# Up projection's two activation parts in one 512-column product, with a third of its weight parts left on VectorE

## The chip, the cores and the metric

The kernel runs on one core of a Trainium2 chip. The metric is device time in microseconds (us) of one execution. Engines are named as in the profile: PE is TensorE's products, PEld its weight loads, DVE is VectorE, ACT is ScalarE, POOL is GpSimd, SP issues most of the DMAs.

## The reference

Two decoder layers on 256 tokens of width 1024, all in float32. Each layer has token mixers, a gated merge, a convolutional feed-forward block and a per-layer embedding. The change sits in the feed-forward block:

```python
def conv_ffn(u, w_up, conv_w, conv_b, w_down):
    up = u @ w_up
    pad = jnp.pad(up, ((0, 0), (CONV_W - 1, 0), (0, 0)))
    length = up.shape[1]
    conv = conv_b + sum(pad[:, j:j + length] * conv_w[j] for j in range(CONV_W))
    gate, val = jnp.split(conv, 2, axis=-1)
    return (jax.nn.gelu(gate, approximate=True) * val) @ w_down

# in each layer, D_MODEL = 1024, D_FF = 2816, CONV_W = 3
h = h + conv_ffn(rms_norm(h, g_ffn_norm[i]), w_up[i], conv_w[i], conv_b[i], w_down[i])
```

So `w_up` is 1024 x 5632, and each of its 5632 output columns is convolved over the tokens with three taps and a bias. The first half goes through a GELU and multiplies the second.

## The kernel before

Every large product is made of three products of the type float32r: an operand x is kept as hi + lo, where hi is x rounded to that type and lo the remainder, and x times w becomes hi(x) hi(w) + lo(x) hi(w) + hi(x) lo(w).

**Weights.** A layer's weights come as 128 chunks of 128 x 1024 numbers (`raw`, 512 KB). `split_hi` makes `wh` on ACT (L159), `split_lo` makes `wl = raw - wh` on DVE (L166), and then the next chunk's DMA is issued on SP. There are 5 `raw` buffers and 7 of each part. `prepare` keeps the parts up to 5 chunks ahead of use; it is called from `tick`, which is called after each group of products, so a chunk's parts stand in the instruction streams of ACT and DVE between the evictions of chunks that are used earlier. Every engine works through its stream in the order written.

**Activations.** A class `HL` holds hi and lo of a [128, 8, 256] operand (k of eight, 256 tokens) in separate tiles.

**Up projection.** It takes chunks 54 to 97 of a layer, 44 chunks: for each of 22 blocks `fb` of 128 columns, one chunk of the gate half (s = 0) and one of the value half (s = 1). A chunk's 8 k give 24 products of 256 columns (L827, L828, L829) into one of 4 PSUM tiles `tp`. Then ACT makes the last tap and the bias (L832), DVE adds the two shifted taps straight from PSUM (L834, twice), ACT applies the GELU to the gate half (L840), DVE multiplies the halves (L841), and ACT and DVE make hi and lo of the result (L846, L847), which the down projection uses as its stationary operand. A PSUM tile is free once the second L834 of its chunk is done, so PE can be at most four chunks ahead of DVE.

**Before it** come the output projection, whose second half ends with the norm of the feed-forward block (`ev_n`: sums of squares on ACT, three small instructions on POOL L265 to L267, two scalings `un` on DVE L783, for each of two token tiles), the transposes `ffn_T` on PE (L789) and the split of `u` (L791, L792). The small product with the embedding's projection runs between these steps. **After it** comes the down projection with 512-column products (L881 to L883).

Of the kernel before, what the change touches and what calls it, by code (L numbers as in the profile page):

```python
# [17 lines left out]
P = 128  # L18
# [90 lines left out]
def decoder_kernel(ctx: ExitStack, tc: tile.TileContext, x, pT, ws, fc, tb, gf, rope, out):  # L109
# [53 lines left out]
    def split_lo():  # L163
        raw = raws.pop(nx["lo"])
        wh, wl = parts[nx["lo"]]
        nc.vector.tensor_sub(wl, raw, wh.bitcast(F32))  # L166
        side.work(dve=1.12)
# [4 lines left out]
    def split_piece(a, n):  # L172
        """Columns a to a + n of the next chunk."""
# [12 lines left out]
    def prepare(n_lo, n_hi):  # L186
        """Have the parts of the chunks before n_lo and n_hi emitted."""
# [65 lines left out]
    def sq_half(ss, hf, tiles=(0, 1)):  # L253
        """ss[hf][:, i] = sum of h^2 / D over half of the columns."""
# [18 lines left out]
    class HL:  # L273
        """fp32r parts hi + lo of [128, 8, 256] operands, stored by halves of the k index."""

        def __init__(self, name, n=2):
            self.h = [b4(name + "h", F32R) for _ in range(n)]
            self.l = [b4(name + "l", F32R) for _ in range(n)]

        def hi(self, k):  # L280
            return self.h[k // 4][:, k % 4, :]

        def lo(self, k):
            return self.l[k // 4][:, k % 4, :]

    def split_T2(srcs, hf, k0, scale, x, between=None):
        """Parts (columns k0, k0 + 1 of half hf of x) of the transpose of two [128, 512] tiles; the scale is
        one for all k or a function of k."""
        hi, lo = x.h[hf][:, k0:k0 + 2, :], x.l[hf][:, k0:k0 + 2, :]
# [58 lines left out]
    def tables(l, t):  # L348
        """Tables of the layer: rope with gains, lambda, sub-norm gain."""
# [30 lines left out]
    def rope_rows(dst, src, n, tabs, i, dup=False):  # L380
        """dst, src [128, n, 64]"""
# [19 lines left out]
    def transposed(srcs, nb, dst):  # L401
        """dst [128, nb, 256] from two token-major [128, nb*128] tiles."""
# [9 lines left out]
    def stacked(q3):  # L412
        """fp32r [128 t, n, 2, 64] of [128 t, n, 64]: the two parts of each head side by side."""
# [6 lines left out]
    def transposed_parts(srcs, dsts):  # L420
        """[128, n, 256] (in tiles of 4) from two stacked [128 t, n, 128]."""
# [20 lines left out]
    for l in range(DEPTH):  # L442
# [120 lines left out]
        def heads_side(pr, nm, is_q):  # L563
            """Rope of eight heads, transposed; 1/rms beside the queries, in the keys."""
# [28 lines left out]
        def maps(qn, product, i, hq, mk):  # L593
            """Four masked score maps, exp'd, [128 t, 4, S]; head 4 hq + 2 m + r."""
# [21 lines left out]
        def ptrans(src, nh, i):  # L616
            """[128 s, nh * blocks, 128 t] of [128 t, nh, S]."""
# [69 lines left out]
        def mixer_a(hq, i):  # L687
# [20 lines left out]
            hi, lo = (t[0][:, 2 * hq:2 * hq + 2, i * P:(i + 1) * P] for t in (x.h, x.l))  # L708
# [61 lines left out]
        pxs = HL("px", 1)  # L770
# [5 lines left out]
        def ev_n(i, acc):  # L776
            """Second half of the columns of a token tile, then its norm for the ffn."""
# [8 lines left out]
        def ffn_T(i, hf):  # L786
# [3 lines left out]
            hi, lo = (t[hf][:, :, i * P:(i + 1) * P] for t in (u.h, u.l))  # L790
            nc.scalar.activation(hi, pt, AF.Copy)  # L791
            nc.vector.tensor_sub(lo, pt, hi.bitcast(F32))  # L792

        for hf in range(2):
# [227 lines left out]
```

## Time and profile before

| | |
|---|---|
| median of 3 timed executions | 800.34 us (798.68 to 802.0) |
| span of the profiled execution | 798.6 us |
| PE busy | 789.2 us, 99% of the span |
| DVE, ACT, POOL busy | 605.8 us (76%), 477.8 us (60%), 63.2 us (8%) |
| mean granted TensorE clock | 1.000 |

The profiled execution is known by its span, from its first to its last instruction; the timed executions lie 0.1 to 3.4 us above that. PE's busy time says that products stood in its pipeline nearly always. How fast they go through is read from the distance between the starts of two of them.

### The profile page before, as it was taken

What the parts mean: (1) busy time and instruction counts of PE and PEld (TensorE: products, weight loads), DVE (VectorE), ACT (ScalarE), POOL (GpSimd) and SP (SyncE); (2) the same over time, 40 slices, a digit from 0 to 9 for tenths busy, and PEclk for the clock granted to TensorE, in tenths of its full rate; (3) what the DMA queues carried; (4) which work ended last, traced back from release to release, by engine and by line L of the source; (5) the groups of instructions that cost most, each with busy time, mean ns of one, the idle gap of its engine ahead of it and who ended that gap; (6) DMA issues with size and microseconds to landing.
All of it is one profiled execution on the core that took longest, in us unless ns stands there. A gap on an engine that the chain in (4) does not pass through costs nothing.

```text
span 798.6 us, 12832 instructions
## 1 busy us (share of the span) xinstructions
PE 789.2 (99%) x4801; PEld 690.7 (86%) x4801; DVE 605.8 (76%) x1084; ACT 477.8 (60%) x843; POOL 63.2 (8%) x87
## 2 busy tenths in 40 slices
PE   8999999999999999999999999999999999999997
PEld 6877887788999999888888778878899999998887
DVE  6988986777888888754687889778688888884643
ACT  6767658366666666553566486575476666663541
POOL 0250300010000000000123212000100000000000
PEclk9999999999999999999999999999999999999999
DMA  8644463574555555656464335445555555567421
GB/s 324 205 158 134 132 211 106 172 235 135 185 185 185 184 185 180 228 172 225 133 201 162 125 121 188 154 132 191 190 160 184 185 185 186 184 190 259 162 102 53
DMA packets 40334, 139.58 MB, mean 175 GB/s; under 512 B 4560, under 2 KB 5968, under 8 KB 40272
## 3 DMA queue, kind: packets, MB, share of 16 engines
q1 hardware_dynamic: 39408, 136.91, 52.0%
q10 hardware_dynamic: 864, 1.84, 0.7%
q8 instruction: 38, 0.62, 0.3%
q14 instruction: 24, 0.20, 0.1%
HBM read 137.69 MB, written 1.05 MB: 174 GB/s over the span
## 4 chain that ended last, share of the span: by engine, by line
PE 93%; DVE 2%; POOL 1%; ACT 1%; DMA 1%; issue 1%; SPq 0%; DVEq 0%; ACTq 0%; POOLq 0%
PE acc L335 12%; PE acc L337 12%; PE acc L336 12%; PE tp L828 11%; PE tp L827 11%; PE tp L829 11%; PE acc L883 5%; PE acc L881 5%; PE acc L882 5%; PE tp L298 2%; PE tp L626 1%; PE tp L634 1%; POOL rq L251 1%; PE tp L705 1%; PE tp L639 1%; PE tp L605 1%
## 5 line engine op out<-in xcount | busy, mean ns | idle before, releaser
L166 DVE TENSOR_TENSOR wl<-raw,wh 128x1024 fp32r<-128x1024 f32 x254 | 306.2, 1219 | 25.9 <-ACT wh L159 25.4
L159 ACT ACTIVATE wh<-raw 128x1024 fp32r<-128x1024 f32 x254 | 264.7, 1057 | 38.8 <-PE acc L883 30.1
L828 PE MATMUL tp<-ul,wh 128*128 128x256 f32 x704 | 199.4, 283 | 0.0
L827 PE MATMUL tp<-uh,wh 128*128 128x256 f32 x704 | 199.4, 283 | 0.0
L829 PE MATMUL tp<-uh,wl 128*128 128x256 f32 x704 | 199.2, 283 | 0.0
L828 PEld LDWEIGHTS tp<-ul,wh 128*128 128x128 f32 x704 | 135.1, 192 | 0.1
L827 PEld LDWEIGHTS tp<-uh,wh 128*128 128x128 f32 x704 | 135.1, 192 | 0.0
L829 PEld LDWEIGHTS tp<-uh,wl 128*128 128x128 f32 x704 | 135.1, 192 | 0.0
L335 PE MATMUL acc<-wh,uh 128*128 128x512 f32 (+1 forms) x336 | 133.7, 398 | 0.0
L337 PE MATMUL acc<-wh,ul 128*128 128x512 f32 (+1 forms) x336 | 130.6, 389 | 0.0
L336 PE MATMUL acc<-wl,uh 128*128 128x512 f32 (+1 forms) x336 | 130.3, 388 | 0.0
L834 DVE SCALAR_TENSOR_TENSOR cv<-tp,fc,cv 128x255 f32<-128x255 f32 (+1 forms) x176 | 84.9, 483 | 40.2 <-ACT cv L832 37.0
L832 ACT ACTIVATE cv<-tp,fc 128x256 f32<-128x256 f32 x88 | 49.6, 564 | 90.0 <-PE tp L829 90.0
L337 PEld LDWEIGHTS acc<-wh,ul 128*128 128x128 f32 x336 | 63.1, 188 | 12.9
L335 PEld LDWEIGHTS acc<-wh,uh 128*128 128x128 f32 x336 | 63.2, 188 | 11.8 <-issue 0.3
L336 PEld LDWEIGHTS acc<-wl,uh 128*128 128x128 f32 x336 | 63.2, 188 | 11.6 <-DVE wl L166 0.2
L881 PE MATMUL acc<-wh,gh 128*128 128x512 f32 x176 | 68.9, 391 | 0.0
L883 PE MATMUL acc<-wh,gl 128*128 128x512 f32 x176 | 68.5, 389 | 0.0
L882 PE MATMUL acc<-wl,gh 128*128 128x512 f32 x176 | 68.5, 389 | 0.0
L265 POOL TENSOR_SCALAR sst<-ss 128x2 f32<-128x2 f32 (+1 forms) x8 | 5.6, 699 | 513.0 <-ACT junk L257 512.9
L611 ACT ACTIVATE pe<-tp,nb,rq 128x256 f32<-128x256 f32 (+1 forms) x64 | 31.8, 523 | 17.4 <-DVE nb L608 13.6
L883 PEld LDWEIGHTS acc<-wh,gl 128*128 128x128 f32 x176 | 33.0, 188 | 6.9
(185 smaller groups left out, 1018.9 us busy)
## 6 DMA issues: line engine op xcount, KB each, us to landing
raw<-ws SPq DMA_DIRECT2D x254, 512.0 KB, 3.4
raw<-ws SPq DMA_DIRECT2D x4, 256.0 KB, 5.0
gb<-gf ACTq DMA_DIRECT2D x2, 512.0 KB, 4.5
h<-x SPq DMA_DIRECT2D x2, 256.0 KB, 4.1
h<-x SPq DMA_DIRECT2D x1, 512.0 KB, 6.4
px<-pT ACTq DMA_DIRECT2D x2, 256.0 KB, 2.6
out<-h SPq DMA_DIRECT2D x2, 256.0 KB, 2.0
out<-h SPq DMA_DIRECT2D x4, 128.0 KB, 1.7
```

The source lines that it names most:

```text
L159: nc.scalar.activation(wh, raw, AF.Copy)
L166: nc.vector.tensor_sub(wl, raw, wh.bitcast(F32))
L335: nc.tensor.matmul(o, a, wh, start=q == 0, stop=False)
L336: nc.tensor.matmul(o, a, wl, start=False, stop=False)
L337: nc.tensor.matmul(o, b, wh, start=False, stop=q == nk - 1)
L827: nc.tensor.matmul(pu, wh[:, k, :], u.hi(k), start=k == 0, stop=False)
L828: nc.tensor.matmul(pu, wh[:, k, :], u.lo(k), start=False, stop=False)
L829: nc.tensor.matmul(pu, wl[:, k, :], u.hi(k), start=False, stop=k == KD - 1)
L834: nc.vector.scalar_tensor_tensor(c[:, sh:], pu[:, :L - sh], w[:, 2 - sh:3 - sh], c[:, sh:], op0=ALU.mult, op1=ALU.add)
L881: nc.tensor.matmul(acc[i], a, wh, start=k == 0, stop=False)
L882: nc.tensor.matmul(acc[i], a, wl, start=False, stop=False)
L883: nc.tensor.matmul(acc[i], b, wh, start=False, stop=k == NF - 1)
```

## The change

`HL` now keeps hi and lo of one k side by side, so that both are one operand of 512 columns (`pair`). In the up projection, the products of `wh` with hi and with lo become one product into a whole PSUM bank: its left half collects the terms of hi, its right half those of lo. The product of `wl` with hi goes on adding to the left half. Then the halves have to be added: ACT copies the right half to SBUF (`cl`), and DVE adds it to the left half, in place in PSUM. The last tap and the bias stay on ACT for the gate half and go to DVE for the value half. Of the 44 chunks of an up projection, the `wl` of 30 are made on POOL and those of 14 stay on DVE. In `ffn_T` each split becomes two, of two k each.

```diff
+    def on_pool(c):
+        return C_UP <= c < C_DN and (c - C_UP) % 3 != 2
...
     def split_lo():
         raw = raws.pop(nx["lo"])
         wh, wl = parts[nx["lo"]]
-        nc.vector.tensor_sub(wl, raw, wh.bitcast(F32))
-        side.work(dve=1.12)
+        if on_pool(nx["lo"] % NCHUNK):
+            nc.gpsimd.tensor_tensor(wl, raw, wh.bitcast(F32), op=ALU.subtract)
+        else:
+            nc.vector.tensor_sub(wl, raw, wh.bitcast(F32))
+            side.work(dve=1.12)
...
     class HL:
-        def __init__(self, name, n=2):
-            self.h = [b4(name + "h", F32R) for _ in range(n)]
-            self.l = [b4(name + "l", F32R) for _ in range(n)]
+        def __init__(self, name, n=KD):
+            self.t = [b4(name, F32R).rearrange("p (k a) t -> p k a t", a=2) for _ in range(n // 2)]
...
+        def pair(self, k):
+            return self.t[k // 2][:, k % 2, :, :]
...
         def ffn_T(i, hf):
...
-            nc.scalar.activation(hi, pt, AF.Copy)
-            nc.vector.tensor_sub(lo, pt, hi.bitcast(F32))
+            for k in (0, 2):
+                hi, lo = u.two(4 * hf + k, slice(i * P, (i + 1) * P))
+                nc.scalar.activation(hi, pt[:, k:k + 2, :], AF.Copy)
+                nc.vector.tensor_sub(lo, pt[:, k:k + 2, :], hi.bitcast(F32))
...
-                pu = ps_tp.tile([P, 512], F32, name="tp")[:, :L]
+                acc = ps_tp.tile([P, 2, L], F32, name="tp")
+                pu = acc[:, 0, :]
                 for k in range(KD):
-                    nc.tensor.matmul(pu, wh[:, k, :], u.hi(k), start=k == 0, stop=False)
-                    nc.tensor.matmul(pu, wh[:, k, :], u.lo(k), start=False, stop=False)
+                    nc.tensor.matmul(acc, wh[:, k, :], u.pair(k), start=k == 0, stop=False)
                     nc.tensor.matmul(pu, wl[:, k, :], u.hi(k), start=False, stop=k == KD - 1)
                 c = sm.tile([P, L], F32, name="cv", **T2)
+                cl = sm.tile([P, L], F32, name="cl", bufs=3)
                 w = cw[:, s * NF + fb, :]
-                nc.scalar.activation(c, pu, AF.Identity, bias=w[:, 3:4], scale=w[:, 2:3])
+                nc.scalar.activation(cl, acc[:, 1, :], AF.Copy)
+                nc.vector.tensor_add(pu, pu, cl)
+                if s:
+                    nc.vector.tensor_scalar(c, pu, w[:, 2:3], w[:, 3:4], op0=ALU.mult, op1=ALU.add)
+                else:
+                    nc.scalar.activation(c, pu, AF.Identity, bias=w[:, 3:4], scale=w[:, 2:3])
```

DVE's stream in the middle of an up projection, one block before: L834 are the taps of one chunk, L841 the product of the halves, L847 the lo part of the block ahead, L166 a weight part.

```order
L834 SCALAR_TENSOR_TENSOR cv<-tp,fc_76,cv 128x255
L834 SCALAR_TENSOR_TENSOR cv<-tp,fc_76,cv 128x254
L847 TENSOR_TENSOR gl<-cv,gh 128x256
L166 TENSOR_TENSOR wl<-raw,wh 128x1024
L834 SCALAR_TENSOR_TENSOR cv<-tp,fc_76,cv 128x255
L834 SCALAR_TENSOR_TENSOR cv<-tp,fc_76,cv 128x254
L166 TENSOR_TENSOR wl<-raw,wh 128x1024
L841 TENSOR_TENSOR cv<-cv 128x256
```

The same block now, one of those with a weight part left (L173): L849 adds the halves, L851 is the value half's last tap, L855 are the shifted taps, L868 the lo part, L862 the product of the halves.

```order
L849 TENSOR_TENSOR tp<-tp,cl 128x256
L855 SCALAR_TENSOR_TENSOR cv<-tp,fc_76,cv 128x255
L855 SCALAR_TENSOR_TENSOR cv<-tp,fc_76,cv 128x254
L868 TENSOR_TENSOR g<-cv,g 128x256
L173 TENSOR_TENSOR wl<-raw,wh 128x1024
L849 TENSOR_TENSOR tp<-tp,cl 128x256
L851 TENSOR_SCALAR cv<-tp,fc_76 128x256
L855 SCALAR_TENSOR_TENSOR cv<-tp,fc_76,cv 128x255
L855 SCALAR_TENSOR_TENSOR cv<-tp,fc_76,cv 128x254
L862 TENSOR_TENSOR cv<-cv 128x256
```

Of the two weight parts of a block 14/22 of one is left on average; two adds and one tap came in. In three blocks one has its part here, one in front of L862, one has none.

ACT's stream in one block now: L848 copies the right half, L853 is the gate half's last tap, L867 the hi part, L163 a weight part, L861 the GELU.

```order
L848 ACTIVATE cl<-tp 128x256
L853 ACTIVATE cv<-tp,fc_76 128x256
L867 ACTIVATE g<-cv 128x256
L163 ACTIVATE wh<-raw 128x1024
L848 ACTIVATE cl<-tp 128x256
L163 ACTIVATE wh<-raw 128x1024
L861 ACTIVATE cv<-cv 128x256
```

Before, each L848 here was an L832, and L853 did not exist. The value half's L848 stands behind a weight part of 1024 columns.

POOL's stream at the start of an up projection, now: L272 to L274 are the norm's three instructions for one token tile, L171 is a weight part.

```order
L272 TENSOR_SCALAR sst<-ss_1835 128x1
L273 TENSOR_TENSOR sst<-sst,ss_1836 128x1
L274 TENSOR_TENSOR rstd<-sst,mhalf 128x1
L171 TENSOR_TENSOR wl<-raw,wh 128x1024
L272 TENSOR_SCALAR sst<-ss_1835 128x1
L273 TENSOR_TENSOR sst<-sst,ss_1836 128x1
L274 TENSOR_TENSOR rstd<-sst,mhalf 128x1
L171 TENSOR_TENSOR wl<-raw,wh 128x1024 x29
```

Before, the six norm instructions (L265 to L267) stood there alone. The 30 weight parts are new: one between the two token tiles, 29 behind.

## Rows read from the trace of the kernel before

**Rows 1.** The page: busy us of each engine, share of the span, instructions.
```profile
PE 789.2 (99%) x4801; PEld 690.7 (86%) x4801; DVE 605.8 (76%) x1084; ACT 477.8 (60%) x843; POOL 63.2 (8%) x87
```
**Rows 2.** The chain that ended last, share of the span by line.
```profile
PE acc L335 12%; PE acc L337 12%; PE acc L336 12%; PE tp L828 11%; PE tp L827 11%; PE tp L829 11%; PE acc L883 5%; PE acc L881 5%; PE acc L882 5%; PE tp L298 2%; PE tp L626 1%; PE tp L634 1%; POOL rq L251 1%; PE tp L705 1%; PE tp L639 1%; PE tp L605 1%
```
**Rows 3.** Both up projections as stretches: busy us (instructions), PEclk, DMA share, GB/s.
```profile
190.00:317.00 127.00, 127.00 (x1058) 126.90 (x1058) 106.31 (x174) 81.78 (x134) 0.00 (x0) 1.00 0.57 186
583.00:710.00 127.00, 127.00 (x1060) 126.92 (x1059) 106.28 (x174) 81.76 (x133) 0.00 (x0) 1.00 0.57 185
```
**Rows 4.** Timeline of PE, up projection: start us, us, instruction.
```profile
230.02 0.28 PE L827 MATMUL tp<-uh,wh 128*128 128x256 f32 x1
...
230.38 0.28 PE L827 MATMUL tp<-uh,wh 128*128 128x256 f32 x1
```
**Rows 5.** Timeline of PE, down projection.
```profile
340.61 0.39 PE L881 MATMUL acc<-wh,gh 128*128 128x512 f32 x1
...
341.29 0.39 PE L881 MATMUL acc<-wh,gh 128*128 128x512 f32 x1
```
**Rows 6.** Groups of DVE by form: busy us, mean ns | idle before.
```profile
L166 DVE TENSOR_TENSOR wl<-raw,wh 128x1024 fp32r<-128x1024 f32 x254 | 306.2, 1219 | 25.9 <-ACT wh L159 25.4 <-issue 0.3
L834 DVE SCALAR_TENSOR_TENSOR cv<-tp,fc,cv 128x255 f32<-128x255 f32 x88 | 42.5, 483 | 37.0 <-ACT cv L832 37.0
L841 DVE TENSOR_TENSOR cv<-cv 128x256 f32<-128x256 f32 x44 | 18.4, 419 | 1.1 <-ACT cv L840 1.1
L847 DVE TENSOR_TENSOR gl<-cv,gh 128x256 fp32r<-128x256 f32 x44 | 18.3, 416 | 1.0 <-ACT gh L846 1.0
L710 DVE TENSOR_TENSOR ol<-tp,oh 128x256 fp32r<-128x256 f32 x8 | 3.4, 424 | 11.6 <-ACT oh L709 11.6
L695 DVE TENSOR_SCALAR pe<-pe,rcp 128x256 f32<-128x256 f32 x16 | 4.6, 349 | 0.1
```
**Rows 7.** Groups of ACT by form.
```profile
L159 ACT ACTIVATE wh<-raw 128x1024 fp32r<-128x1024 f32 x254 | 264.7, 1057 | 38.8 <-PE acc L883 30.1 <-DMA raw<-ws 8.6
L832 ACT ACTIVATE cv<-tp,fc 128x256 f32<-128x256 f32 x88 | 49.6, 564 | 90.0 <-PE tp L829 90.0
L840 ACT ACTIVATE cv<-cv 128x256 f32<-128x256 f32 x44 | 17.8, 405 | 0.0
L709 ACT ACTIVATE oh<-tp 128x256 fp32r<-128x256 f32 x8 | 3.1, 384 | 12.0 <-PE tp L705 12.0
```
**Rows 8.** Timeline of ACT and DVE, up projection, one chunk: [idle before <-releaser].
```profile
230.58 0.57 ACT L832 ACTIVATE cv<-tp,fc 128x256 f32<-128x256 f32 x1 [1.06 <-PE tp L829]
...
231.18 1.00 DVE L834 SCALAR_TENSOR_TENSOR cv<-tp,fc,cv 128x255 f32<-128x255 f32 x2 [0.41 <-ACT cv L832]
...
232.10 1.22 DVE L166 TENSOR_TENSOR wl<-raw,wh 128x1024 fp32r<-128x1024 f32 x1
...
233.23 0.42 DVE L841 TENSOR_TENSOR cv<-cv 128x256 f32<-128x256 f32 x1
```
**Rows 9.** Timeline of DVE and POOL at the end of the output projection.
```profile
172.02 1.22 DVE L166 TENSOR_TENSOR wl<-raw,wh 128x1024 fp32r<-128x1024 f32 x1
...
172.27 1.02 POOL L265 TENSOR_SCALAR sst<-ss 128x1 f32<-128x1 f32 x1 [74.84 <-ACT junk L257]
```
**Rows 10.** Timeline of POOL in the attention stage.
```profile
82.32 0.20 POOL L250 TENSOR_SCALAR pw<-hss 128x8 f32<-128x8 f32 x1 [26.94 <-DVE hss L398]
```
**Rows 11.** Groups of POOL by form.
```profile
L242 POOL CAST identr<-ident 128x128 fp32r<-128x128 f32 x1 | 0.3, 294 | 0.0
...
L250 POOL TENSOR_SCALAR pw<-oss 128x2 f32<-128x2 f32 x8 | 1.5, 192 | 8.1 <-DVE oss L670 6.5 <-ACT pt L627 1.2
```
**Rows 12.** Timeline of DVE and PE ahead of the first up projection.
```profile
185.40 1.42 DVE L783 SCALAR_TENSOR_TENSOR un<-h,rstd,gb 128x512 f32<-128x512 f32 x2 [1.77 <-POOL rstd L267]
...
189.51 0.60 PE L789 MATMUL tp<-ident,un 128*128 128x128 f32 x4
```
**Rows 13.** DMA issues: KB each, median us from issue to landing.
```profile
raw<-ws SPq DMA_DIRECT2D x254, 512.0 KB, 3.4
```

More of the change, by code (lines that the diff above doesn't have):

```diff
@@ L273, in decoder_kernel, with two @@
     class HL:
-        def __init__(self, name, n=2):
-            self.h = [b4(name + "h", F32R) for _ in range(n)]
-            self.l = [b4(name + "l", F32R) for _ in range(n)]
+        def __init__(self, name, n=KD):
+            self.t = [b4(name, F32R).rearrange("p (k a) t -> p k a t", a=2) for _ in range(n // 2)]
         def hi(self, k):
-            return self.h[k // 4][:, k % 4, :]
+            return self.t[k // 2][:, k % 2, 0, :]
         def lo(self, k):
-            return self.l[k // 4][:, k % 4, :]
+            return self.t[k // 2][:, k % 2, 1, :]
+        def pair(self, k):
+            return self.t[k // 2][:, k % 2, :, :]
+        def two(self, k, cols=slice(0, L)):
+            return (self.t[k // 2][:, :, a, cols] for a in range(2))
     def split_T2(srcs, hf, k0, scale, x, between=None):
-        hi, lo = x.h[hf][:, k0:k0 + 2, :], x.l[hf][:, k0:k0 + 2, :]
+        hi, lo = x.two(4 * hf + k0)
         n = 1 if callable(scale) else 2
@@ L707, in mixer_a @@
             x = o_parts()
-            hi, lo = (t[0][:, 2 * hq:2 * hq + 2, i * P:(i + 1) * P] for t in (x.h, x.l))
+            hi, lo = x.two(2 * hq, slice(i * P, (i + 1) * P))
             nc.scalar.activation(hi, po, AF.Copy)
@@ L769, in decoder_kernel @@
         ss = new_ss()
-        pxs = HL("px", 1)
+        pxs = HL("px", 2)
         u = HL("u")
@@ L789, in ffn_T @@
                 nc.tensor.transpose(pt[:, k, :], un[i][:, hf, k * P:(k + 1) * P], ident)
-            hi, lo = (t[hf][:, :, i * P:(i + 1) * P] for t in (u.h, u.l))
-            nc.scalar.activation(hi, pt, AF.Copy)
-            nc.vector.tensor_sub(lo, pt, hi.bitcast(F32))
+            for k in (0, 2):
+                hi, lo = u.two(4 * hf + k, slice(i * P, (i + 1) * P))
+                nc.scalar.activation(hi, pt[:, k:k + 2, :], AF.Copy)
+                nc.vector.tensor_sub(lo, pt[:, k:k + 2, :], hi.bitcast(F32))
         for hf in range(2):
@@ L800, in decoder_kernel @@
             if hf:
-                nc.scalar.activation(pxs.h[0][:, 0:2, :], px, AF.Copy)
-                nc.vector.tensor_sub(pxs.l[0][:, 0:2, :], px, pxs.h[0][:, 0:2, :].bitcast(F32))
+                pxh, pxl = pxs.two(0)
+                nc.scalar.activation(pxh, px, AF.Copy)
+                nc.vector.tensor_sub(pxl, px, pxh.bitcast(F32))
                 gemm_a(m, range(KD), stream(l, C_OUT + 4), 512, ev_n, {13: lambda: ffn_T(0, 0)}, outer=KD)
@@ L836, in decoder_kernel @@
                 cc.append(c)
-                side.work(pe=2.6)
-                side.work(dve=0.8, act=0.8)
+                side.work(pe=2.5)
+                side.work(dve=1.4 + 0.3 * s, act=1.1 - 0.5 * s)
                 tick()
@@ L841, in decoder_kernel, with parts_g @@
             nc.vector.tensor_mul(cc[1], cc[1], cc[0])
-            if fb % 4 == 0:
-                gx.append(HL("g", 1))
-            def parts_g(c=cc[1], ghi=gx[-1].hi(fb % 4), glo=gx[-1].lo(fb % 4)):
+            if fb % 2 == 0:
+                gx.append(HL("g", 2))
+            def parts_g(c=cc[1], ghi=gx[-1].hi(fb % 2), glo=gx[-1].lo(fb % 2)):
                 nc.scalar.activation(ghi, c, AF.Copy)
@@ L878, in decoder_kernel @@
                 for i in range(2):
-                    a = gx[k // 4].hi(k % 4)[:, i * P:(i + 1) * P]
-                    b = gx[k // 4].lo(k % 4)[:, i * P:(i + 1) * P]
+                    a = gx[k // 2].hi(k % 2)[:, i * P:(i + 1) * P]
+                    b = gx[k // 2].lo(k % 2)[:, i * P:(i + 1) * P]
                     nc.tensor.matmul(acc[i], a, wh, start=k == 0, stop=False)
```

## The prediction

> **What bounds the kernel now.** I read the page first: PE is busy 99% of the span [rows 1]. That says little of its pace, so I went to the chain that ended last: nearly all of it is products, and the three lines of the up projection have 11% each, a third of the time [rows 2]. The two stretches of it, 127 us each, show PE busy throughout at full clock, DVE at 106 us of 127, ACT at 82, POOL at nothing [rows 3]. So these stages go at PE's pace. It is read from starts: three 256-column products take 0.36 us, 120 ns each [rows 4]; three 512-column ones of the down projection take 0.68 us, 226.7 ns each [rows 5]. A chunk of 24 products takes 2.88 us, a block of two 5.76. In it, ACT idles 1.06 us until PE is done with the chunk, and DVE then 0.41 us until ACT is [rows 8]: both wait for PE, not PE for them. That is what the change may spend.
>
> **PE's part.** Doubling the columns adds 106.7 ns, which is 256 columns at 2.4 GHz; so each product carries 13.3 ns that do not depend on columns. Per k, two products of 120 become one of 226.7 and the third stays: 346.7 instead of 360. For 8 k and 88 chunks that is 704 x 13.3 = **9.4 us less**, and a chunk takes 2.77 us, a block 5.55, a layer's up projection 122. The operand's weights are loaded beside a longer product than before, so I add nothing for loads. The Trainium skill ("TensorE: Matmul & The Clock Gate", Back-to-back issue gap) gives columns over 2.4 GHz plus 2.5 ns as the gap between isolated warm products; by it 704 x 2.5 = 1.8 us would be saved. Rows 4 and 5 do not agree with that gap, and the sum goes by the rows.
>
> **DVE's block without POOL.** Lengths overlap a little from one instruction to the next, so I take distances between starts: the two taps 0.92, a weight part 1.13 [rows 8], and for 256-column ones without a wait the length less 0.08, so 0.34 [rows 6]. New in it are two adds from PSUM, nearest row L710, 424 ns, and one last tap: 349 ns is a scaling from SBUF, 483 one with two inputs [rows 6], I take 0.42. Neither row writes PSUM; I come back to that. Handing over between engines, or between an instruction and one of the same engine that needs it, costs 0.03 to 0.04: L832 ends at 231.15, the tap starts at 231.18 [rows 8].
> Gate half: add 0.42, then DVE stands while ACT makes the last tap, 0.56 [rows 7] and two handovers, 0.07; taps 0.91; lo part 0.34. That is 2.30.
> Value half: add 0.46, last tap 0.46, taps 0.91, multiply 0.34: 2.17.
> Weight parts: 14/22 x 1.13 = 0.72.
> Also, ACT reaches the value half's copy (0.384 by L709) only behind hi part and weight part [rows 7]: 0.45 + 0.47 + 0.30 + 0.95 + 0.38 = 2.55 us after the gate half's add began, while DVE is there after 2.30. So it waits 0.29 in the two of three blocks that have no weight part in front: 0.19. Sum: **5.38 of 5.55 us**. ACT's own work (two weight parts, two copies, last tap, GELU, hi part) is under 4.3 us. DVE fits, with 0.17 us per block, 3.7 us per layer; before, its waits for ACT alone were 0.8 per block [rows 8]. Besides, four PSUM tiles let DVE fall behind: three chunks of 2.77 are 8.3 us, less the 2.5 us that a chunk's chain takes anyway, 5.8 us per layer.
>
> **POOL's part.** 30 weight parts per layer. No row shows a long two-input instruction on POOL. A cast of 128 columns takes 294 ns, one of 2 columns 192 [rows 11]: 0.81 ns per column, 1.02 us for 1024 read once. Two operands read in turn: 0.19 + 2 x 0.83 = 1.85 us. I keep 1.02 and 1.85 as bounds and take 1.85, since there are two operands. (The Trainium skill, "GPSIMD Engine Reference", Elementwise side-by-side, measured 4497 ns for 2048 columns, an estimate of 2.25 us here; no run here shows it, and the sum below would come to about 840 us.) POOL then has 30 x 1.85 = 55 us of work in 122, 45%.
>
> **Where POOL and DVE meet.** A POOL instruction issued at 172.27, 0.25 us into a weight part of DVE that ran from 172.02 to 173.24, took 1.02 us and ended at 173.29, just behind it [rows 9]. One of the same kind on eight times the columns, right behind the reduction on DVE that it had waited for, took 0.20 [rows 10]. So while DVE streams two inputs from SBUF, POOL does not get through. Whether DVE stands likewise while POOL reads, no row shows: POOL's reads are too short. I forecast that it does. The Trainium skill ("SBUF — State Buffer", Who interferes with whom) says so: DVE with two SBUF inputs and a reading GpSimd exclude each other for whole instructions, whoever comes first. Rows 9 agree for the one order.
> DVE has 22 multiplies, 22 lo parts and 14 weight parts per layer with two SBUF inputs (the taps and adds have one in PSUM): 58. If each meets a busy POOL 45% of the time and then waits half of 1.85, that is 58 x 0.42 = 24.4 us per layer. Off it go 3.7 and 5.8 us from above, and 1.9 where the lo part's wait falls into the 0.29 that DVE waits for the copy anyway (22 x 2/3 x 0.29 x 0.45). **13.0 us per layer remain, 26 in all**: multiply and taps behind the caught instruction come late, PSUM tiles come free late, and PE stands. Both bounds: at 1.02 us the waits are 58 x 0.25 x 0.51 = 7.4 us and vanish in the slack. And arrivals are not random, since POOL starts when ACT ends a weight part: with a quarter or three quarters of a part left on average, the waits are 12 or 37 us, and 0.8 or 25 remain per layer.
>
> **What I cost at nothing.** `ffn_T` issues 4 more instructions on ACT and DVE each per layer, some 0.2 us apiece; PE works on the embedding's product then, and without that cover they cost 2 to 3 us in all. The first POOL weight part stands between the two norms: its 1.85 us fit before the second sum of squares. The second one can hold up the last `un`: done at 186.82, used at 189.51 [rows 12], 2.7 us of cover; uncovered, 1.85 per layer. `raw` buffers are held up to 1 us longer, against a landing of 3.4 [rows 13] and five buffers in 13.9 us.
>
> **Sum.** 800.3 - 9.4 + 26 = **817 us**, against the median; the profiled span of 798.6 would become 815.
>
> **Rivals.**
> *Main, 0.52:* POOL's reads hold up DVE: 792 to 841 by the bounds on the waits, 817.
> *PE's pace is reached, 0.33, the other side:* DVE goes on while POOL reads, or POOL's part is near 1 us. For it: DVE's lengths under a POOL instruction are those without, 1.22 in rows 9. Against: they were all first, or met short ones. Then 800.3 - 9.4 = 791. It decides at waits of (3.7 + 5.8 + 1.9) / 58 = 0.2 us per two-input instruction.
> *Both nearly cancel, 0.08:* 4 to 7 us per layer remain: 797 to 804.
> *POOL is the bound, 0.04:* from 122 / 30 = 4.1 us per part on; at 5 us a stage takes 150, so 800 + 2 x 23 = 846.
> *DVE is too slow by itself, 0.03:* an add that writes PSUM at 0.7 instead of 0.42 costs 12 us per layer against 9.5 of slack; 796, and 0.1 more per add is 9 us more.
>
> Half a per cent, 4 us, is about what these timings tell from no change. Faster: 0.33 and a little of the main case's lower end, 0.34; same 0.10; slower 0.56. The range, 789 to 842, takes in PE's pace and the main case's upper bound; outside lie a bound POOL and worse contention.
>
> **What would show it.** Starts of 512- and 256-column products 0.347 us apart in pairs. POOL's L171 near 1.85 us when no two-input DVE instruction stands before it. DVE's L862, L868 and L173 either longer than 0.42 and 1.22 or starting late right behind an L171; PE idle in front of L843, released by DVE's L855, 13 us per layer. I am wrong if PE goes through both stages in 122 us: then POOL's reads do not hold up DVE, or too little. I am wrong about the size if L171 takes clearly more than 1.85 us, or if always the same instruction is caught.

## The result, and the profile after

The changed kernel takes **824.61 us** (median of 4 executions, 823.86 to 825.59) against 800.22 us of the kernel before in the same session: 1.0311 times as long, 95% interval 1.0295 to 1.0327, or 24.4 us more. The forecast was 817 us in a range of 789 to 842, with 56% on slower. The profiled execution took 825.59 us and has a span of 823.8 us, 25.2 us more than that of before.

Where they lie is read first, from three starts in each layer: the first up product, the first down product, and the last down product of `wh` with hi (L881 before, L902 in after, L896 in e5_pair_alone; two more products start in the 0.45 us behind it). In us:

| kernel | to first up product | up | down | between | up | down | tail | span |
|---|---|---|---|---|---|---|---|---|
| before | 189.9 | 126.9 | 60.1 | 206.3 | 126.9 | 60.1 | 28.4 | 798.6 |
| after | 197.5 | 129.5 | 63.9 | 212.5 | 129.6 | 62.4 | 28.5 | 823.8 |
| e5_pair_alone | 189.9 | 123.7 | 60.1 | 205.2 | 123.7 | 60.1 | 28.4 | 791.1 |

The stages that the change aims at lose 2.6 us each. The down projections lose 6.1 together, and **more than half of the loss, 13.8 us, stands ahead of the up projections**: 7.6 and 6.2 us. Of the 7.6, 1.9 are there before GpSimd has its first weight part: the addition L791 ahead of the norm begins at 178.72, that of before (L778) at 176.85. The windows at the start, before and then after (columns as in [rows 3]), show where they come from:

```profile
5.00:15.00 10.00, 8.82 (x47) 7.14 (x46) 7.52 (x14) 7.32 (x14) 0.00 (x0) 1.00 1.01 370
5.00:15.00 10.00, 7.88 (x38) 6.74 (x37) 5.67 (x11) 6.01 (x13) 0.00 (x0) 0.83 0.98 363
```

In this execution of after, PE stood 2.12 us for a piece of `h`, against 1.18 before, and the granted clock was at its lower level behind that, so that it averaged 0.83. The profiles of e3, e8, e9 and e11 have the same 0.83 there, and those of e1, e5 and e10 have 1.00, with the same program up to this point. So these 1.9 us go with the execution and not with the change.

The page of after, its busy line and the chain that ended last by line, which answer to [rows 1, 2]:

```profile
PE 795.5 (97%) x4097; PEld 656.9 (80%) x4097; DVE 627.4 (76%) x1164; ACT 478.2 (58%) x895; POOL 221.8 (27%) x147
PE acc L348 11%; PE acc L350 11%; PE acc L349 11%; DVE cv L855 7%; PE acc L903 4%; PE acc L904 4%; PE acc L902 4%; DVE tp L849 4%; DVE wl L173 3%; DVE cv L851 3%; DVE cv L862 2%; ACT cv L853 2%; DMA raw<-ws 2%; ACT wh L163 2%; DVE g L868 2%
```

Before, three lines of up products had 33% of the chain. Now no up product is among its lines, and DVE's taps L855 lead that stage: DVE sets its pace. Groups of after by form, from the norm to the start of the down projection of the first layer:

```profile
L173 DVE TENSOR_TENSOR wl<-raw,wh 128x1024 fp32r<-128x1024 f32 x19 | 32.1, 1695 | 0.0
L851 DVE TENSOR_SCALAR cv<-tp,fc 128x256 f32<-128x256 f32 x21 | 11.4, 544 | 0.8
L868 DVE TENSOR_TENSOR g<-cv,g 128x256 fp32r<-128x256 f32 x20 | 9.8, 489 | 0.0
L862 DVE TENSOR_TENSOR cv<-cv 128x256 f32<-128x256 f32 x20 | 8.7, 437 | 1.4
L796 DVE SCALAR_TENSOR_TENSOR un<-h,rstd,gb 128x512 f32<-128x512 f32 x4 | 7.0, 1790 | 3.5 <-POOL rstd L274 3.5
...
L171 POOL TENSOR_TENSOR wl<-raw,wh 128x1024 fp32r<-128x1024 f32 x30 | 79.1, 2645 | 57.6 <-ACT wh L163 52.5 <-PE tp L843 2.7 <-PE tp L844 2.5
```

The instructions of DVE with two SBUF inputs got longer: L173 by 0.48 us over the 1.219 of [rows 6], `un` to a mean of 1.79 from 0.75:

```profile
L783 DVE SCALAR_TENSOR_TENSOR un<-h,rstd,gb 128x512 f32<-128x512 f32 x8 | 5.7, 750 | 7.1 <-POOL rstd L267 7.1
```

That row is from before. The holds add up to 19 x 0.48 + 20 x 0.07 + 20 x 0.02 = 10.9 us of longer instructions in an up projection, and 4.2 in a norm. The taps and the add L849, which have one input in PSUM, take the same with and without GpSimd's reads (0.482 and 0.43 us, here and in e3_no_pool). A caught weight part in the timeline of after:

```profile
241.62 2.40 POOL L171 TENSOR_TENSOR wl<-raw,wh 128x1024 fp32r<-128x1024 f32 x1 [1.21 <-ACT wh L163]
241.68 1.00 DVE L855 SCALAR_TENSOR_TENSOR cv<-tp,fc,cv 128x255 f32<-128x255 f32 x2
242.60 2.51 DVE L173 TENSOR_TENSOR wl<-raw,wh 128x1024 fp32r<-128x1024 f32 x1
245.03 0.41 DVE L862 TENSOR_TENSOR cv<-cv 128x256 f32<-128x256 f32 x1
...
245.82 0.56 ACT L853 ACTIVATE cv<-tp,fc 128x256 f32<-128x256 f32 x1 [3.70 <-DVE tp L849]
```

GpSimd's part ends at 244.02, and L173 at 245.11, 1.09 later. So it stood for the whole rest of that part, 1.42 us, and then ran through. The taps in between ran beside GpSimd at their usual length.

What PE met in the stage is in two rows of the page of after:

```profile
L843 PE MATMUL tp<-u,wh 128*128 128x512 f32 x704 | 248.8, 398 | 0.0
L844 PE MATMUL tp<-u,wl 128*128 128x256 f32 x704 | 199.1, 283 | 7.3 <-DVE wl L173 6.9
```

PE never stands in front of L843, the first of which opens a chunk's PSUM tile. It stands in front of L844, for DVE's own weight parts, which come late: from the 24th chunk on, in every third one.

Now the norm, in the timeline of after:

```profile
181.11 2.36 POOL L171 TENSOR_TENSOR wl<-raw,wh 128x1024 fp32r<-128x1024 f32 x1
181.18 3.50 DVE L796 SCALAR_TENSOR_TENSOR un<-h,rstd,gb 128x512 f32<-128x512 f32 x2 [1.77 <-POOL rstd L274]
...
184.16 0.63 PE L802 MATMUL tp<-ident,un 128*128 128x128 f32 x4 [2.08 <-DVE un L796]
...
192.34 0.84 PE L802 MATMUL tp<-ident,un 128*128 128x128 f32 x4 [2.27 <-DVE un L796]
192.83 0.78 PE L348 MATMUL acc<-wh,px 128*128 128x512 f32 x1
193.40 0.63 PE L349 MATMUL acc<-wl,px 128*128 128x512 f32 x1
193.83 0.63 PE L350 MATMUL acc<-wh,px 128*128 128x512 f32 x1
```

GpSimd's part starts 0.07 us ahead of `un`, since it is the next instruction behind the 1/rms on GpSimd's own stream, while DVE needs the handover. So the first `un` waits for all of it, the transposes come 2.1 us late, and the same happens for the second token tile at 189.28. Behind the second wait the products of 512 columns start 0.42 us apart instead of 0.23; the windows of after show the clock:

```profile
184.00:190.00 6.00, 5.84 (x29) 4.65 (x29) 2.86 (x6) 2.71 (x6) 1.50 (x4) 1.00 0.26 87
190.00:198.00 8.00, 5.73 (x24) 4.70 (x24) 5.50 (x7) 3.17 (x7) 2.83 (x2) 0.79 0.28 77
```

After PE had stood for 2.08 and then 2.27 us, the granted clock fell to its lower level, 1.2 GHz, for some seven products, which is 7 x 0.2 = 1.4 us more. Less the 0.18 that PE stood there before, 2.1 + 2.1 + 1.4 = 5.6 us per layer.

### The profile page after: what moved, and what is told of

It is laid out like the page before. It is cut to its first block, busy times and chain, and to the rows that moved or that the text cites. A ratio compares the mean times of both kernels' runs of the same rounds, so it can differ in the third digit from the quotient of the medians.

```text
span 823.8 us, 11709 instructions
## 1 busy us (share of the span) xinstructions
PE 795.5 (97%) x4097; PEld 656.9 (80%) x4097; DVE 627.4 (76%) x1164; ACT 478.2 (58%) x895; POOL 221.8 (27%) x147
## 4 chain that ended last, share of the span: by engine, by line
PE 56%; DVE 25%; issue 9%; ACT 6%; POOL 2%; DMA 2%; SPq 0%; DVEq 0%; ACTq 0%; POOLq 0%
PE acc L348 11%; PE acc L350 11%; PE acc L349 11%; DVE cv L855 7%; PE acc L903 4%; PE acc L904 4%; PE acc L902 4%; DVE tp L849 4%; DVE wl L173 3%; DVE cv L851 3%; DVE cv L862 2%; ACT cv L853 2%; DMA raw<-ws 2%; ACT wh L163 2%; DVE g L868 2%
## 5 line engine op out<-in xcount | busy, mean ns | idle before, releaser
L163 ACT ACTIVATE wh<-raw 128x1024 fp32r<-128x1024 f32 x254 | 264.8, 1058 | 31.1 <-PE acc L904 20.0
L173 DVE TENSOR_TENSOR wl<-raw,wh 128x1024 fp32r<-128x1024 f32 x194 | 251.2, 1312 | 18.4 <-ACT wh L163 18.1
L843 PE MATMUL tp<-u,wh 128*128 128x512 f32 x704 | 248.8, 398 | 0.0
L844 PE MATMUL tp<-u,wl 128*128 128x256 f32 x704 | 199.1, 283 | 7.3 <-DVE wl L173 6.9
L171 POOL TENSOR_TENSOR wl<-raw,wh 128x1024 fp32r<-128x1024 f32 x60 | 158.2, 2645 | 115.3 <-ACT wh L163 105.1
L843 PEld LDWEIGHTS tp<-u,wh 128*128 128x128 f32 x704 | 132.2, 188 | 31.5
L844 PEld LDWEIGHTS tp<-u,wl 128*128 128x128 f32 x704 | 133.0, 189 | 11.7 <-DVE wl L173 11.7
L348 PE MATMUL acc<-wh,u 128*128 128x512 f32 (+1 forms) x336 | 134.3, 400 | 0.0
L350 PE MATMUL acc<-wh,u 128*128 128x512 f32 (+1 forms) x336 | 131.2, 390 | 0.0
L349 PE MATMUL acc<-wl,u 128*128 128x512 f32 (+1 forms) x336 | 131.0, 390 | 0.0
L855 DVE SCALAR_TENSOR_TENSOR cv<-tp,fc,cv 128x255 f32<-128x255 f32 (+1 forms) x176 | 84.9, 482 | 32.6 <-ACT cv L853 27.9
L853 ACT ACTIVATE cv<-tp,fc 128x256 f32<-128x256 f32 x44 | 24.8, 565 | 105.0 <-DVE tp L849 105.0
L272 POOL TENSOR_SCALAR sst<-ss 128x2 f32<-128x2 f32 (+1 forms) x8 | 7.1, 886 | 263.2 <-ACT junk L264 263.0
L350 PEld LDWEIGHTS acc<-wh,u 128*128 128x128 f32 x336 | 63.5, 189 | 13.0
L348 PEld LDWEIGHTS acc<-wh,u 128*128 128x128 f32 x336 | 63.6, 189 | 11.8 <-issue 0.3
L349 PEld LDWEIGHTS acc<-wl,u 128*128 128x128 f32 x336 | 63.7, 189 | 11.7 <-DVE wl L173 0.2
L903 PE MATMUL acc<-wl,g 128*128 128x512 f32 x176 | 69.5, 395 | 3.3 <-DVE wl L173 2.7
L902 PE MATMUL acc<-wh,g 128*128 128x512 f32 x176 | 68.9, 392 | 0.0
L904 PE MATMUL acc<-wh,g 128*128 128x512 f32 x176 | 68.6, 390 | 0.0
L849 DVE TENSOR_TENSOR tp<-tp,cl 128x256 f32<-128x256 f32 x88 | 37.5, 427 | 7.2 <-ACT cl L848 7.2
```

The source lines that it names most:

```text
L163: nc.scalar.activation(wh, raw, AF.Copy)
L171: nc.gpsimd.tensor_tensor(wl, raw, wh.bitcast(F32), op=ALU.subtract)
L348: nc.tensor.matmul(o, a, wh, start=q == 0, stop=False)
L349: nc.tensor.matmul(o, a, wl, start=False, stop=False)
L350: nc.tensor.matmul(o, b, wh, start=False, stop=q == nk - 1)
L843: nc.tensor.matmul(acc, wh[:, k, :], u.pair(k), start=k == 0, stop=False)
```

## The experiments

All ratios are against the kernel before on the same chip, with 95% intervals. "Block" is the steady distance of two GELUs of ACT, one per block of two chunks.

**e1_norm_clear: no GpSimd part in the norm.**

```diff
-        return C_UP <= c < C_DN and (c - C_UP) % 3 != 2
+        return C_UP + 2 <= c < C_DN and (c - C_UP) % 3 != 2
```

> The changed kernel, but the weight parts of chunks 54 and 55, the two that POOL makes around the norm, are left to DVE; POOL keeps 28 per layer. Theory A (a POOL part that reads holds up a DVE instruction with two SBUF inputs): the scalings un go back from 2.84 to 0.75 us, PE's idle time at the transposes goes, and the 5.6 and 7.4 us that the two norms lost come back: 824.6 - 13 = 812. Theory B (the norm is late because ffn_T's splits were doubled, or DVE's stage is too long by itself): un is not the cause, under 3 us come back, 822 to 825.

813.58 us, 1.0181 (1.0161 to 1.0201). `un` took 0.75 us again, PE reached the first up projection at 190.1 us and the second 205.2 us behind the first down stage: 7.4 and 7.3 less than after. That loss goes with the norm's two parts, as theory A has it; 5.6 of it are in the rows above, and 1.4 came back as longer up stages (130.9 and 131.0 us): the first chunk now waits for the last parts of `u` (4.42 us, 2.90 in after), a wait that in after was over before the stage began. In the first layer 1.9 stood at the start, and in the second, kernels that are the same in this stretch lie 1.1 apart (205.2 in e5, 206.3 in e7).

**e2_pool_only: the kernel before, with the 30 parts on GpSimd and nothing else changed.**

```diff
+        c = nx["lo"] % NCHUNK
+        if C_UP <= c < C_DN and (c - C_UP) % 3 != 2:
+            nc.gpsimd.tensor_tensor(wl, raw, wh.bitcast(F32), op=ALU.subtract)
```

> The kernel before, with nothing changed but 30 of 44 weight parts per up projection moved to POOL; no pair, no add. Theory A: the norms lose their 13 us here too, though DVE has less work than before; in the up projection DVE has some 2.4 us of room per block now, so PE keeps 2.88 us per chunk: 800.2 + 13 = 813. Theory B (DVE's added work alone made the change slow): POOL only relieves DVE, 798 to 801.

810.6 us, 1.015 (1.0114 to 1.0187). All of it stands ahead of the up projections (+6.0 and +4.6). These took 126.9 us as before, although their multiplies averaged 1.45 us: 26 us of holds a layer, in the multiplies and the lo parts, with 30 weight parts off DVE, stay behind PE's pace. A hold costs only where DVE has no slack.

**e4_all_pool: 42 of the 44 parts on GpSimd.**

```diff
+        return C_UP + 2 <= c < C_DN
```

> The changed kernel with chunks 54 and 55 on DVE and the other 42 weight parts of an up projection on POOL. POOL then has two parts of 2.41 us per block, DVE only the multiply and the lo part with two SBUF inputs. Theory A: norms as in the run above, no DVE weight part that waits or is waited for; each multiply or lo part can still be caught, by at most 2.4 us: between 796 (all caught ones fall into time that DVE has) and 812. If waits per caught instruction add up as in my forecast (half of each part, two thirds and more of the time), it is over 815. Theory B: DVE is relieved of 28 parts, 796.

862.63 us, 1.0786 (1.0768 to 1.0804): a miss. The timeline of this kernel, the pattern of every block:

```profile
230.26 4.77 POOL L171 TENSOR_TENSOR wl<-raw,wh 128x1024 fp32r<-128x1024 f32 x2 [2.56 <-ACT wh L163]
...
232.64 2.67 DVE L862 TENSOR_TENSOR cv<-cv 128x256 f32<-128x256 f32 x1
```

Two parts run back to back on GpSimd, and the multiply, which has no slack behind it, meets the start of the second one each time (2.33 us on average). A block takes 7.3 us, with no weight part of the steady stage on DVE. Here PE does stand in front of L843, released by DVE's taps L855: 46.8 us in both layers. Averages over arrivals, mine included, are no guide here.

**e5_pair_alone: the paired product by itself.** All parts on DVE; the two halves are not added, so the terms of lo(x) are left out of the sum.

```diff
-        return C_UP <= c < C_DN and (c - C_UP) % 3 != 2
+        return False
...
-                nc.scalar.activation(cl, acc[:, 1, :], AF.Copy)
-                nc.vector.tensor_add(pu, pu, cl)
...
+                nc.scalar.activation(c, pu, AF.Identity, bias=w[:, 3:4], scale=w[:, 2:3])
...
-                side.work(dve=1.4 + 0.3 * s, act=1.1 - 0.5 * s)
+                side.work(dve=0.8, act=0.8)
```

> The pair of columns alone: all weight parts on DVE, no copy of the right half and no add, last tap on ACT as before. It leaves out the lo half of the activations from the sum. It shows what PE's part is worth. My forecast's 346.7 ns per k would give 800.2 - 9.4 = 790.8. The 353.3 ns that the changed kernel's timeline shows (starts of ten pairs, 3.18 us for nine) would give 800.2 - 704 x 0.0067 = 795.5, and then the longer distance is the mixed stream's own; at 346.7 it came from waiting in the changed kernel.

795.37 us, 0.9943 (0.9917 to 0.9969). Chunks start 2.773 us apart, 346.7 ns per k, as forecast; but the stage gains 3.2 us, not 4.7. The first chunk takes 4.40 us, and the timeline of this kernel says why:

```profile
192.64 0.50 PE L843 MATMUL tp<-u,wh 128*128 128x512 f32 x1 [1.06 <-DVE u L806]
```

PE stands for the last parts of `u`, which `ffn_T` now makes in twice as many instructions that wait for one another: first chunk 4.40 - 2.77 = 1.63 us above the others, against 3.08 - 2.88 = 0.20 before.

**e3_no_pool: the change with all weight parts on DVE.**

```diff
-        return C_UP <= c < C_DN and (c - C_UP) % 3 != 2
+        return False
...
-                side.work(dve=1.4 + 0.3 * s, act=1.1 - 0.5 * s)
+                side.work(dve=0.8, act=0.8)
```

`side.work` holds estimates of DVE's and ACT's time per chunk, by which the program places its side work; here and in e5 they are those of the kernel before.

> The changed kernel with all weight parts on DVE (none on GpSimd; the planner is told 0.8 us of DVE and of ACT per up chunk, as in the pair-alone run). Both theories: no `un` is held up, so the norms cost what they cost before (190 us to the first up product, 205 to 206 between the layers). Theory A (what the change loses comes from GpSimd's reads holding up DVE, and without GpSimd DVE has too much of its own): a block of two chunks asks 5.38 + 16/22 x 2 x 0.57 us more = 5.38 + (44 - 14) / 22 x 1.13 = 6.9 us of DVE against 5.55 of PE; an up projection takes 144 to 154 us, the kernel 835 to 855 us. Rival B (DVE's added work is small and is hidden; only GpSimd costs): up projections near 124, the kernel 795 to 800 us.

849.66 us, 1.0619 (1.0603 to 1.0635). The block is 6.87 us in steady state, 6.9 expected. Taking off 30/22 of a weight part, 1.54, leaves 5.33 us for DVE's block in the changed kernel without GpSimd's reads, where I had 5.38. This is an estimate by subtraction; no run has 14 parts on DVE and none on GpSimd. After has 6.13. So by this estimate the add alone does not break PE's pace there, and what meeting GpSimd adds does.

**e6_pieces and e7_pieces_clear: each GpSimd part in four pieces; e7 also without those in the norm.**

```diff
+            for a in range(0, CW, 256):
+                b = slice(a, a + 256)
+                nc.gpsimd.tensor_tensor(wl[:, b], raw[:, b], wh[:, b].bitcast(F32), op=ALU.subtract)
```

> The changed kernel with each weight part on GpSimd made as four instructions of 256 columns instead of one of 1024. Theory A (a two-input instruction of DVE waits until the one GpSimd instruction that reads is through, and no longer): a hold lasts at most 0.19 + 256 x 2.2 / 1024 = 0.75 us instead of 2.4. `un` falls from 1.79 us to 0.75 to 1.5 us, DVE's weight parts L173 from 1.31 to 1.15 to 1.25, the up projections to 124 to 127 us, the norms to within 2 us of before: 796 to 806 us. Rival B (DVE and GpSimd share by time read, not by instruction): GpSimd's reads add up to as much as before, `un` stays near 1.8 us, and the time stays at 820 to 828 us. Rival C (DVE now slips in between the pieces, each piece of GpSimd waits for a DVE instruction in turn, and the weight parts on GpSimd come late): PE waits for GpSimd in the up stages, over 828 us.

> As e6_pieces, with the first two chunks of the up projection on DVE, so that GpSimd has no weight part in the norm ahead of the ffn. Theory A: norms as before (190 and 205 to 206), up projections 124 to 127, the start of the down projection 60 to 62: 793 to 801 us, the part of the e6_pieces gain that the norm still held coming on top (0 to 6 us below e6_pieces). Rival B (holds go by time read): as e1_norm_clear, 812 to 816 us. Rival C: over 816 us.

818.61 us, 1.0233 (1.0215 to 1.0252), and 818.38 us, 1.0226 (1.0209 to 1.0243). Timeline and groups of e6_pieces:

```profile
179.76 3.71 POOL L173 TENSOR_TENSOR wl<-raw,wh 128x256 fp32r<-128x256 f32 x4
179.82 2.35 DVE L798 SCALAR_TENSOR_TENSOR un<-h,rstd,gb 128x512 f32<-128x512 f32 x2 [1.77 <-POOL rstd L276]
```

```profile
L175 DVE TENSOR_TENSOR wl<-raw,wh 128x1024 fp32r<-128x1024 f32 x17 | 22.9, 1354 | 0.0
L864 DVE TENSOR_TENSOR cv<-cv 128x256 f32<-128x256 f32 x20 | 17.3, 865 | 1.4
```

In the norm theory A held: `un` fell to 1.2 us and the norms to 191.3 and 206.1. In the up stage it failed: the block is 6.23 us, more than with whole parts. A hold is shorter, but GpSimd's part takes longer (2.84 us by itself), and now the multiply is caught in nearly every block (0.865). Cutting up the part moves the waits and does not shorten the block. With the norm clear it is slower than whole parts: 818.38 us in e7 against 813.58 in e1. Both times miss theory A's forecasts.

**e8_down_pool: the down projection's first two parts on GpSimd too.**

```diff
+        return C_UP <= c < C_DN and (c - C_UP) % 3 != 2 or c in (C_DN, C_DN + 1)
```

> The changed kernel with the weight parts of the first two chunks of the down projection on GpSimd too. Theory A (the down projection starts late because its first weight parts on DVE stand behind the work that DVE still owes to the last up chunks): PE finds these parts ready, the stages from the first down product to the last product of the down projection fall from 63.9 and 62.4 us to 60 to 61.5, and the time from 824.6 to 818 to 821 us. Rival B (the last up chunks hold up the down projection in another way, through the `g` parts or the raw buffers, or GpSimd's two more parts hold up DVE by as much as they take off it): the down stages stay at 62 to 64 us, the time at 823 to 827 us.

831.34 us, 1.0394 (1.037 to 1.0417): theory A missed. The down stages took 68.9 and 62.8 us. PE found the first parts ready and stood later, for the next part of DVE. Timeline of e8_down_pool, first layer:

```profile
342.42 0.29 DVE L376 TENSOR_TENSOR rt_ka<-rp,tbl 128x128 f32<-128x128 f32 x1 [2.89 <-DMA tbl<-tb]
...
345.59 0.63 PE L903 MATMUL acc<-wl,g 128*128 128x512 f32 x1 [4.23 <-DVE wl L173]
```

There DVE reached the tables of the next layer before their DMA had landed, and the weight part stood behind them. So what DVE owes at the end of the up stage seems to be all its work, not the first two parts.

**e9_gate and e10_value: 21 parts on GpSimd, of the gate or of the value halves.**

```diff
+        return C_UP + 2 <= c < C_DN and (c - C_UP) % 2 == 0    # e9_gate; == 1 in e10_value
```

> The changed kernel with other chunks on GpSimd: the weight parts of the gate halves (21 of 44 chunks of a layer), none in the norm; the value halves and the first two chunks are DVE's. DVE's own work per block of two chunks is 6.87 us (measured with no part on GpSimd) less 21/22 x 1.13, so 5.79. Theory A (a two-input instruction of DVE that meets GpSimd waits, and which one it meets is set by the order in which the engines free each other, the same in each block): this run and the next one, with the same number of parts on GpSimd, differ by more than 5 us. Rival B (arrivals are as good as random, so only the number of parts counts): 0.80 us of waits per block for 30 parts, so 0.56 for 21, a block takes 6.35 us, the kernel 813 to 820 us, and both runs agree within 3 us.

> The changed kernel with the weight parts of the value halves on GpSimd instead (21 of 44 chunks of a layer), none in the norm; the gate halves and the first two chunks are DVE's. Theory A (phase-locked waits): more than 5 us away from the run with the gate halves, on either side; with no wait at all a block takes 5.79 us and the kernel 800 to 804 us, and with one instruction in each block caught for half a part or a whole one it takes 6.99 or 8.2 us and the kernel about 826 or 850. Rival B (random arrivals): 813 to 820 us, within 3 us of the run with the gate halves.

863.06 us, 1.0793 (1.0773 to 1.0813), and 807.39 us, 1.0097 (1.008 to 1.0113): 56 us apart with the same work on each engine. 47.9 us of that lie in the up stages. Some of the rest is in the norms: in e9 GpSimd's first part catches the last `un` of each layer (2.92 and 2.91 us), in e10 none. Timeline of e9_gate:

```profile
260.88 2.39 POOL L171 TENSOR_TENSOR wl<-raw,wh 128x1024 fp32r<-128x1024 f32 x1 [4.91 <-ACT wh L163]
...
261.86 2.49 DVE L173 TENSOR_TENSOR wl<-raw,wh 128x1024 fp32r<-128x1024 f32 x1
```

Timeline of e10_value:

```profile
262.80 1.22 DVE L173 TENSOR_TENSOR wl<-raw,wh 128x1024 fp32r<-128x1024 f32 x1
262.85 3.44 POOL L171 TENSOR_TENSOR wl<-raw,wh 128x1024 fp32r<-128x1024 f32 x1 [2.56 <-ACT wh L163]
```

In e9 GpSimd is first by 1 us in every steady block, and DVE's part takes 2.50 us, 19 of 19 in each layer: a block of 7.30. In e10 DVE is first by 0.05 us, keeps its 1.22, and GpSimd's part takes 3.43 instead of 2.39, which nobody waits for: 5.98, 0.19 above the 5.79 without any hold. Which instruction is first decides, and the order repeats from block to block. Theory A has the two runs more than 5 us apart, as they are, but e10 lies between its 800 to 804 us and the 813 to 820 of rival B; its down projections take 6.0 us more than before's.

**e11_fill and e12_fill_down: e10_value with the parts of `g` moved into DVE's wait for the gate half's last tap.** e12 also gives GpSimd the down projection's second chunk.

```diff
+                late = g_last.pop() if g_last and not s else None
+                if late:
+                    nc.scalar.activation(late[1], late[0], AF.Copy)
                 nc.vector.tensor_add(pu, pu, cl)
...
+                if late:
+                    nc.vector.tensor_sub(late[2], late[0], late[1].bitcast(F32))
                 for sh in (1, 2):
```

> The run with the value halves on GpSimd (e10_value), and the two parts of `g` of a block moved in the program: they stand between the next gate half's add and its taps, so ACT makes the hi part ahead of the gate half's last tap, and DVE the lo part while ACT makes that tap. A block of e10_value takes 5.98 us of DVE, 0.63 of which DVE stands in front of the gate half's taps, released by ACT. Theory A (DVE sets the pace of these stages, and the 0.42 us lo part fits into that wait): a block takes 5.55 to 5.65 us, which is PE's pace, DVE's wait for ACT there falls from 0.63 to 0.2 us, the up projections take 123.5 to 126 us, the down projections 60 to 62, the kernel 793 to 800 us. Rival B (the phase of GpSimd's part moves with it, and another two-input instruction is caught in each block): a block takes 6.2 to 7.3 us and the kernel 812 to 850 us. Rival C (the block is paced by something else, ACT's order or the held-up GpSimd): 805 to 808 us as e10_value.

> As e11_fill, with the weight part of the down projection's second chunk on GpSimd too, which goes on with the pattern of every second chunk for one chunk more. Theory A (DVE owes less at the end of the up projection, and its first parts for the down projection come earlier): 0 to 3 us below e11_fill, from the down stages. Rival B (as with two chunks more on GpSimd in e8_down_pool, PE only waits for the next part of DVE instead): the same as e11_fill within 1 us, or slower.

798.48 us, **0.9977 (0.9963 to 0.999)**, and 800.58 us, 0.9999 (0.9986 to 1.0012). Timeline and the windows of e11_fill:

```profile
261.06 0.57 ACT L857 ACTIVATE cv<-tp,fc 128x256 f32<-128x256 f32 x1
261.17 0.43 DVE L859 TENSOR_TENSOR g<-cv,g 128x256 fp32r<-128x256 f32 x1
...
261.66 1.00 DVE L862 SCALAR_TENSOR_TENSOR cv<-tp,fc,cv 128x255 f32<-128x255 f32 x2
```

```profile
200.00:320.00 120.00, 120.00 (x680) 103.97 (x680) 110.49 (x212) 83.33 (x150) 68.05 (x20) 1.00 0.51 183
```

The lo part L859 runs while ACT makes the tap, the block falls from 5.98 to 5.65 us, and PE is busy throughout. Up stages take 126.0 us, down stages 60.1 as before. This is theory A, at the slow end: PE's own pace is 2.83 us per chunk here, 2.77 in e5. e12 gains nothing on it (rival B). e11 is the one version of the whole computation that beats the kernel before, by 0.2%, which is less than I called measurable; its interval leaves out 1. It is 26 us below the change as made.

## Why the prediction was right, and where its steps were not

**Direction and mechanism: right.** GpSimd's reads hold up DVE; e1, e9 and e10 show it in both orders. The Trainium skill ("SBUF — State Buffer", Who interferes with whom) has this rule, whoever starts first keeps the shared ports for the whole instruction, and that a DVE instruction with at most one SBUF input is free of it. These runs agree: 181.11 and 262.80 above for the two orders, 0.482 us for the taps beside GpSimd.

**PE's part, -9.4 us: right in the pace, not in what comes of it.** 2.773 us per chunk in e5 is the forecast. `ffn_T`, costed at nothing, takes 1.63 - 0.20 = 1.4 us of it per layer, which is the 2 to 3 us in all that I named for the case without cover: 4.7 - 1.4 = 3.3, and e5 gains 3.2. In after, PE also goes at 353 ns per k for more than half of the first stage, from 197.5 to 271 us.

**DVE's block without GpSimd: 5.38 forecast, 5.33 by e3.** The last tap L851 takes 0.544 us where I took 0.42; the pieces were off by more than their sum. The 5.33 is itself a difference and not a measured block.

**GpSimd's part, 1.85 us: mis-sized.** 2.36 to 2.41 by itself, 2.65 with what DVE holds up, above my upper bound: a short cast on GpSimd was no row to scale from. The Trainium skill's figure ("GPSIMD Engine Reference", Elementwise side-by-side), an estimate of 2.25 us, was nearer.

**The waits, 24.4 us per layer: the term's size was off, and its working was wrong.** The holds came to 10.9 us of longer instructions per layer. A block is 6.13 - 5.33 = 0.80 longer, 17.6 us per layer; besides the holds, 3.6 of it are waits of DVE for ACT's copy (L849), the rest I did not assign. Taking off the slack, (5.55 - 5.33) x 22 = 4.8, and the 5.8 of the PSUM tiles as I did, 7.0 us remain where I had 13.0 (DVE's wait for the copy, which I took off apart, is already in the block). The loss against e5 is 5.8 to 5.9 in the stage (5.3 to 5.4 of chunks that wait in front of L844, 2.0 to 2.1 of PE's slower pace, less 1.5 of the first chunk, whose wait for `u` is over before the stage in after) and, as the next point says, 2.3 to 3.8 behind it. I had let instructions arrive at random; e9 and e10 differ by 56 us on the same count of instructions, so no average could have given the size. "If always the same instruction is caught" was named as what would make it wrong, and that is what happened: the pattern repeats every three blocks.

**From DVE to PE: the wrong wait.** I had PSUM tiles coming free late, and named PE idle in front of L843, released by L855, 13 us per layer, as the sign. In after that wait is 0.0. PE stood in front of L844 for DVE's late weight parts, 7.3 us in both layers together. Tiles were what PE waited for in e4, where DVE makes none of these parts. The room itself was near my 5.8: PE goes 23 chunks without a stop, an estimate of 11.5 x (6.13 - 5.65) = 5.5 us.

**The down projection: not in the prediction.** DVE can fall behind PE without stopping it, which I booked as slack of the four PSUM tiles. It is lent, not given: PE ends the up stage while DVE still owes the last blocks, and the down projection's weight parts stand behind them. The timeline of after:

```profile
334.42 0.50 PE L903 MATMUL acc<-wl,g 128*128 128x512 f32 x1 [0.77 <-DVE wl L173]
```

3.8 and 2.3 us more than before, and 2.2 to 3.8 in e1 and e10 too. The first layer has one wait more, 1.22 us at 341.8, for the weight part that stands behind the next layer's tables on DVE. Where DVE keeps up (e5, e11) the stage takes 60.1 us. e8 tried to show that the first two parts alone are the matter and did not: its layer without the tables took 62.8, like after.

**The held-up `un`, costed at nothing: the step that failed.** I had the first GpSimd part between the two norms, with room before the second sum of squares, and gave the last `un` 2.7 us of cover [rows 12], 1.85 us per layer without it. The cover was read at the wrong place: the products at 189.51 take the second half of that `un`, and those of its first half already stood for it in the timeline of before:

```profile
186.30 0.63 PE L789 MATMUL tp<-ident,un 128*128 128x128 f32 x4 [0.18 <-DVE un L783]
```

In fact both parts start directly in front of an `un`, and PE stood 2.08 and 2.27 us, against 0.18 before; then came the slower clock: 5.6 us by the rows of the first layer, 6.2 by the second layer of before and after (there the granted clock fell behind both waits, 0.66 from 588 to 593 and from 598 to 603), 7.3 by e1, of which 1.4 only move the wait for `u`. Cover at one place said nothing of the other, where the transposes are due at once. This is the largest term that the forecast put at nothing.

**The sum:** e5 791.1; up stages 5.8 + 5.9; down 6.1; ahead of the up stages 14.9 against e5 (7.6 + 7.3, with the 1.9 and the 1.1 that are not the change's); tail 0.1: 823.9, and the span is 823.8. These are differences of the two traces, stage by stage, so they add up whatever the cause. That the forecast came within 8 us is luck: of its 26 us for the waits 11.7 came in the up stages, 14.3 too many, and 21.0 were left out, 14.9 ahead of the up stages and 6.1 behind them.

## What to carry to other kernels

Before giving GpSimd an instruction that reads SBUF, list DVE's two-input SBUF instructions that follow the same releaser: the order of the two starts, here 0.07 us one way and 0.05 the other, decides who pays, and it repeats in every iteration, so go through one period by hand instead of averaging. Slack in a ring of buffers is a loan that the next stage pays back. And look for an engine's own waits, such as DVE's 0.63 us for ACT, and move independent work into them: that alone was worth 0.33 us per block, more than the paired product's 0.21.

## What the hardware showed that was not expected

At a granted clock of 1.00, PE goes through the same pairs of products at two paces. Timeline of PE, three pairs in e5_pair_alone, then three in after:

```profile
254.64 0.39 PE L843 MATMUL tp<-u,wh 128*128 128x512 f32 x1
...
255.68 0.40 PE L843 MATMUL tp<-u,wh 128*128 128x512 f32 x1
```

```profile
254.84 0.40 PE L843 MATMUL tp<-u,wh 128*128 128x512 f32 x1
...
255.90 0.40 PE L843 MATMUL tp<-u,wh 128*128 128x512 f32 x1
```

1.04 and 1.06 us; over whole stages, 2.773 us per chunk in e5 and 2.827 in e11, so 346.7 and 353.3 ns per k, 2.3 us per layer. Each pace holds for a long stretch with a fixed pattern of distances; after shows both, and the pace changes where PE has stood. GpSimd being busy or not makes no difference to it (353.3 ns in both cases in e11). What sets it stays open.
